# Summed weight blocks of a two-level FFN product: accumulating transfers into the SBUF chunk in place of sums staged in DRAM

## The chip, the cores and the metric

The kernel runs on one core of a Trainium2 chip. The metric is the device time of one execution in microseconds (us). Before the change it is 1157.83 us (median of 3 runs, 1157.72 to 1158.13).

## The reference, cut to what matters

One layer of a hybrid decoder for 576 tokens (64 new ones of 8 sequences and 512 of a prompt, side by side in one tile): two recurrent branches, a cross-attention, and a SwiGLU FFN. The change touches only how the FFN's input weights arrive:

```
xn = rms_norm(x, g[4])                          # 576 x 1024
gate, up = jnp.split(xn @ w_ffn_in, 2, axis=-1) # w_ffn_in: 1024 x 5632, each half 1024 x 2816
x = x + rms_norm((jax.nn.silu(gate) * up) @ w_ffn_out, g[5])
```

All matrix products are float32 work done as three matmuls on parts of the operands: a weight is split into a high part (`whi`, by ScalarE) and the rest (`wlo`, by VectorE), and so are the activations.

## The kernel before, in words

Weights come through one stream. `w_cols` and `w_blocks` register the chunks in the order in which they will be used; `w_dma` fetches a chunk from DRAM into one of five `wraw` buffers (128 x 1024 float32, 512 KB) by transfers that SyncE issues (L187; the trace shows them at L185); `w_prep` or `w_part` splits it into `whi` and `wlo` (4 buffers each). In the stage around the change, `run_steps` splits the chunk that stands three behind the one in use. SyncE has its own instruction stream, so a fetch waits for nothing but its buffer: chunk n goes out when chunk n-5 has been split.

Column block j is 128 columns of gate and 128 of up, 22 blocks in all. The first 7 (`NB`) are computed plainly. For the other 15, `ffn_pair` computes gate and up for both halves of the tokens (288 columns L, 288 columns R) with seven products in place of eight, in the manner of Strassen and Winograd. Each product takes four 128 x 128 weight blocks, thus 12 matmuls on 288 columns (L1395 to L1397). The weights of a product are EG, OG, EU, OU (even and odd row blocks of gate or up), or a sum of those: s1 = EU + OU, s2 = EG + EU + OU, s3 = EG + EU, s4 = EG + OG + EU + OU. The seven products come in the order EG, s1, s2, OG, s3, s4, OU; each needs 256 KB of weights, and two products in a row share a chunk. Below, a *pair* is a chunk with its two products. Blocks 7 to 13 make 49 products in 25 pairs (part 1), blocks 14 to 21 make 56 in 28 pairs (part 2). Ahead of each part stand eight steps of `ffo_part`, the output product on the columns of the part before, during which the first chunks of the part are fetched and split. In these stages the order on TensorE, ScalarE and VectorE is as written in the code.

The sums s1 to s4 are made earlier in DRAM: 32 transfers of 960 KB (`sum_task`, L557) that GpSimd issues between the steps of the recurrent branches, from 35 us to 385 us. A "copy" writes a sum's first term, an "add" accumulates another (`accum_op`). 16 tiny GpSimd copies into `small` (L758, L779) hold GpSimd's queue to the pace of the steps. In the FFN, `block` then fetches a finished sum from DRAM as it fetches any other block.

GpSimd's DMA queue works in order: a transfer whose wait isn't met holds back all that stand behind it.

Of the kernel before, what the change touches and what calls it, by code (L numbers as in the profile page):

```python
# [9 lines left out]
F32 = mybir.dt.float32  # L10
F32R = mybir.dt.float32r
AF = mybir.ActivationFunctionType
ALU = mybir.AluOpType
# [8 lines left out]
DFF = 2816  # L22
# [5 lines left out]
NB = 7  # L28
# [24 lines left out]
def decoder_step(  # L53
# [7 lines left out]
    nc = tc.nc  # L61
    PE, ACT, DVE, POOL = nc.tensor, nc.scalar, nc.vector, nc.gpsimd
# [38 lines left out]
    def split(hi, lo, src):  # L101
        ACT.copy(hi, src)  # L102
        DVE.tensor_sub(lo, src, f(hi))  # L103
# [74 lines left out]
    def w_dma(upto):  # L178
        while ptr["dma"] <= min(upto, len(wsrc) - 1):
            i = ptr["dma"]  # L180
            srcs, nk, ncol, _ = wsrc[i]
            t = wraw_p.tile([128, 1024], F32, tag="wraw", name="wraw")
            n = nk * ncol // len(srcs)
            for j, src in enumerate(srcs):
                nc.sync.dma_start(out=t[:, j * n:(j + 1) * n].rearrange("p (k c) -> p k c", c=ncol), in_=src)  # L185
            raw[i] = t
            ptr["dma"] += 1  # L187

# [2 lines left out]
    def w_part(i, b, dma_ahead=2):  # L191

        if i >= len(wsrc) or (b == 0 and ptr["prep"] > i) or (b == 1 and i not in parts):
            return
        assert b or ptr["prep"] == i
        w_dma(i + dma_ahead)
        _, nk, ncol, as_is = wsrc[i]
        if as_is or nk * ncol < 1024:
            if b == 0:
                w_prep(i)  # L200
            return
        if b == 0:
            ptr["prep"] += 1
            t = raw.pop(i)
            hi = whi_p.tile([128, 1024], F32R, tag="whi", name="whi")
            lo = wlo_p.tile([128, 1024], F32R, tag="wlo", name="wlo")
            parts[i] = t, hi, lo
            ready[i] = hi.rearrange("p (k c) -> p k c", c=ncol), lo.rearrange("p (k c) -> p k c", c=ncol)
        t, hi, lo = parts[i] if b == 0 else parts.pop(i)
        s = slice(b * 512, b * 512 + 512)  # L210
        split(hi[:, s], lo[:, s], t[:, s])
# [30 lines left out]
    def drain(budget=None):  # L242
        spent = 0
        while bg and (budget is None or spent < budget):
            c, fn = bg.popleft()
            if fn is NEXT:
                if budget is not None:
                    return
                continue
            with tc.high_priority(offset=PRIO):  # L250
                fn()
            spent += c

    def step(w, pe, post=None, budget=4000, prep=True):
        steps.append((w, pe, post, budget, prep))

    def run_steps():
        nextw = 0
        manual = ExitStack()
        by_hand = False  # L260
        for w, pe, post, budget, prep in steps:
            if w:
                nextw = w[-1] + 1
            if prep in ("pair", "hand"):
                if not by_hand:
                    by_hand = True
                    drain(None)
                    w_prep(nextw - 1 + 2)
                    manual.enter_context(tc.manual_schedule(engines={PE.engine, ACT.engine, DVE.engine}))
                pe(*[ready.pop(i) for i in w])  # L270
                soon, late = post or (None, None)
                if soon:
                    soon()
                if prep == "pair":
                    w_part(nextw - 1 + 3, 0 if w else 1)
                else:
                    w_prep(nextw - 1 + 3)
                if late:
                    late()
                continue  # L280
            if not prep:
                pe()
            else:
                w_prep((w[0] if w else nextw) + 3)
                pe(*[ready.pop(i) for i in w])
            if post:
                post()
            drain(budget)
        manual.close()
# [13 lines left out]
    small = cst.tile([128, 80], F32, name="small")  # L303
# [237 lines left out]
        return g  # L541

    sums = {n: tc.dram_tile([512, DFF - NB * 128], F32, name=f"sum_{n}") for n in ("s1", "s2", "s3", "s4")}

    def sum_task(op, n, src, i):
        def go():
            r = slice(i * 128, i * 128 + 128)
            if src in sums:  # L550
                a = sums[src][r, :]
            else:
                k = 2 * i + (src[0] == "O")
                c = (src[1] == "U") * DFF
                a = w_ffn_in[0][k * 128:(k + 1) * 128, c + NB * 128:c + DFF]
            kw = {"accum_op": ALU.add} if op == "add" else {}
            tc.keep_in_program_order(nc.gpsimd.dma_start(out=sums[n][r, :], in_=a, **kw))  # L557
        return go

    sum_tasks = deque(  # L560
        sum_task(op, n, src, i)
        for stage in ((("copy", "s1", "EU"), ("copy", "s3", "EG")), (("add", "s1", "OU"), ("add", "s3", "EU")),
                      (("copy", "s2", "s3"),), (("add", "s2", "OU"),), (("copy", "s4", "s2"),), (("add", "s4", "OG"),))
        for op, n, src in stage for i in range(4))

    def sum_step():
        if sum_tasks:
            step([], sum_tasks.popleft(), budget=0)


    h_h, h_l, vv = [None] * KT, [None] * KT, [None] * KT
    box = {}

# [142 lines left out]
    for c in range(KT):  # L716
        def wi(sec):
            return [w_cols(w_in[0], 0, KT, sec * D + c * 128, 128)]
        if c == 0:
            wi(3), wi(1)  # L720
            step([1], startup, lambda: (in_u(0)[1](), in_hc(0)[1](), softplus()), budget=0, prep=False)
        else:
            step(wi(3), *in_u(c), budget=0)
            step(wi(1), *in_hc(c), budget=3000)
        if c:
            sum_step()
        step(wi(2), *in_hh(c), budget=2000)
        if c:
            sum_step()
        step([], *in_gate(c), budget=2000)  # L730
        step(wi(0), *in_hb(c), budget=9000)
        if c:
            sum_step()


    vs_h, vs_l, z1 = [None] * KT, [None] * KT, [None] * KT
# [12 lines left out]
    def br_rnn(n):  # L749
        def pe(W):  # L750
            box["yr"] = mmt()
            gemm2(box["yr"], W, full(h_h, h_l))

        def post():
            t = box.pop("sgs")
            DVE.tensor_mul(both(t), both(t), box.pop("yr")[:, :, :HN])
            z1[n] = t
            POOL.tensor_copy(small[:, n:n + 1], t[:, 0:1])  # L758
            vs_h[n], vs_l[n] = new(F32R), new(F32R)
            split(vs_h[n][:, :T], vs_l[n][:, :T], vv[n][:, :T])  # L760
            free(vv[n])
            if n == 0:
                free(gd, gr_a, gr_x)
            if n == KT - 1:
                free(h_h, h_l)
        return pe, post
# [3 lines left out]
    def br_conv(n):  # L770
        def pe(W):
            box["yc"] = mmt()
            gemm2(box["yc"], W, full(vs_h, vs_l))

        def post():
            t = box.pop("sgs")
            DVE.tensor_mul(both(t), both(t), box.pop("yc")[:, :, :HN])
            DVE.tensor_add(t[:, :T], t[:, :T], z1[n][:, :T])
            POOL.tensor_copy(small[:, n:n + 1], t[:, 0:1])  # L779
            z_h[n], z_l[n] = new(F32R), new(F32R)  # L780
            split(z_h[n][:, :T], z_l[n][:, :T], t[:, :T])
            free(t, z1[n])
            if n == KT - 1:
                free(vs_h, vs_l, xn_h, xn_l)
        return pe, post
# [18 lines left out]
    for n in range(KT):  # L804
        step([w_cols(w_in[0], 0, KT, 5 * D + n * 128, 128)], *br_gate(n, "r"))
        step([w_cols(w_rnn_out[0], 0, KT, n * 128, 128)], *br_rnn(n))
        if n == 1:
            step([], state_out)
        sum_step()
    for n in range(KT):  # L810
        step([w_cols(w_in[0], 0, KT, 4 * D + n * 128, 128)], *br_gate(n, "c"))
        step([w_cols(w_conv_out[0], 0, KT, n * 128, 128)], *br_conv(n))
        sum_step()
    assert not sum_tasks


    fb = [[None] * 2 for _ in range(4)]
# [201 lines left out]
    for h in (h0, h1):  # L1019
        for n in range(KT):  # L1020
            step([w_cols(w_mix_out[0], 0, KT, n * 128, 128)], *proj_half(n, fullh(z_h, z_l), h, 1, after_mix),
                 budget=BUD["mix"])
# [337 lines left out]
    def ffn_half(j, up, h):  # L1360
# [15 lines left out]
            free(t)  # L1376
        return pe, post

    def block(name, j):
        if name in sums:  # L1380
            src = sums[name][:, (j - NB) * 128:(j - NB + 1) * 128].rearrange("(k p) c -> p k c", p=128)
        else:
            c = (name[1] == "U") * DFF + j * 128
            src = w_ffn_in[0][:, c:c + 128].rearrange("(k e p) c -> e p k c", p=128, e=2)[name[0] == "O"]
        return src

    FF = {}

# [354 lines left out]
```

## Time and profile before

| | |
|---|---|
| median of 3 runs | 1157.83 us (1157.72 to 1158.13) |
| profiled execution | 1157.59 us, of which the profile's span 1155.8 us |
| TensorE busy | 1134.3 us, 98% of the span |
| VectorE, ScalarE, GpSimd busy | 58%, 52%, 13% |
| chain that ended last | TensorE 94% |
| DMA, SyncE's queue (q1) | 249812 packets, 149.95 MB, 43.6% of 16 engines' time |
| DMA, GpSimd's queue (q0) | 6144 packets, 38.50 MB, 13.0% |

Matmuls are pipelined: one that the profile shows with 295 ns starts 132 ns after the one before. The pace of TensorE is therefore read from the starts, not from the durations. Transfers show twice: as the short time in which they are issued, and as the time "to landing", from issue until the semaphore says that all is in place. GpSimd's issue time of a transfer isn't counted in its busy time.

### The profile page before, as it was taken

The page shows a single profiled execution, that of the slowest core. Times are in us where ns is not written, and L with a number is a line of the kernel's source. Part 1 is how long each engine was busy: PE and PEld are TensorE (multiplying, and loading weights), DVE is VectorE, ACT ScalarE, POOL GpSimd, SP SyncE. Part 2 cuts the span into 40 slices and gives each one's busy share as a digit, 9 for nine tenths or more (in the row PEclk, how much of TensorE's full clock was granted, in tenths as well). Part 3 has the DMA queues.
Part 4 walks back from the last instruction along what each step waited for, and adds up shares of the span by engine and source line. Part 5 has one row for each costly group of instructions (what it writes and reads, how often), then busy time and mean ns, then how long its engine had stood idle before and what let it go on. Part 6 is the DMA issues. An engine that isn't in the chain of part 4 may idle for free.

```text
span 1155.8 us, 21040 instructions
## 1 busy us (share of the span) xinstructions
PE 1134.3 (98%) x8524; PEld 1113.9 (96%) x8524; DVE 675.0 (58%) x1082; ACT 603.2 (52%) x1030; POOL 146.9 (13%) x301
## 2 busy tenths in 40 slices
PE   6999999999999999999999999999999999999996
PEld 4999999999999999999998899999999999999996
DVE  6666666652223335698767777989314663466535
ACT  5665566652122225666557778775325552255543
POOL 4433333212001000022210000000000000000000
PEclk9999999999999999999999999999999999999999
DMA  7556787567547546567675585565444553455702
GB/s 226 171 163 191 178 186 163 177 160 170 173 141 164 147 123 187 147 193 227 196 227 189 192 274 165 155 200 164 129 126 131 164 150 107 118 164 166 227 2 83
DMA packets 256859, 191.13 MB, mean 165 GB/s; under 512 B 9432, under 2 KB 241896, under 8 KB 256634
## 3 DMA queue, kind: packets, MB, share of 16 engines
q1 hardware_dynamic: 249812, 149.95, 43.6%
q0 software_dynamic: 6144, 38.50, 13.0%
q8 instruction: 67, 1.10, 0.4%
q10 hardware_dynamic: 806, 1.34, 0.3%
q14 instruction: 30, 0.25, 0.1%
HBM read 180.36 MB, written 40.85 MB: 191 GB/s over the span
## 4 chain that ended last, share of the span: by engine, by line
PE 94%; DVE 2%; ACT 1%; DMA 1%; issue 1%; POOL 0%; SPq 0%; DVEq 0%; ACTq 0%
PE mm L107 23%; PE mm L108 23%; PE mm L106 23%; PE aux L1397 4%; PE aux L1396 4%; PE aux L1395 4%; PE aux L1225 1%; PE aux L1209 1%; PE aux L106 1%; PE aux L107 1%; PE aux L108 1%; PE mm L1397 1%; PE mm L1396 1%; PE mm L1395 1%; DMA wraw<-in_w_in_dram 1%
## 5 line engine op out<-in xcount | busy, mean ns | idle before, releaser
L106 PE MATMUL mm<-u,whi 128*128 128x288 f32 (+2 forms) x2032 | 605.3, 298 | 0.6 <-ACT u L458 0.6
L107 PE MATMUL mm<-u,whi 128*128 128x288 f32 (+2 forms) x2032 | 601.7, 296 | 0.5 <-DVE u L103 0.5
L108 PE MATMUL mm<-u,wlo 128*128 128x288 f32 (+2 forms) x2032 | 601.7, 296 | 0.2 <-POOL wlo L431 0.2
L103 DVE TENSOR_TENSOR wlo<-wraw,whi 128x1024 fp32r<-128x1024 f32 (+2 forms) x294 | 304.0, 1035 | 215.5 <-ACT whi L102 209.1
L102 ACT CAST whi<-wraw 128x1024 fp32r<-128x1024 f32 (+2 forms) x294 | 261.1, 898 | 286.6 <-PE mm L107 216.6
L107 PEld LDWEIGHTS mm<-u,whi 128*128 128x128 f32 x2032 | 384.5, 189 | 2.4 <-DVE u L103 1.3
L106 PEld LDWEIGHTS mm<-u,whi 128*128 128x128 f32 x2032 | 384.3, 189 | 2.2 <-ACT u L458 1.2
L108 PEld LDWEIGHTS mm<-u,wlo 128*128 128x128 f32 x2032 | 384.0, 189 | 0.8 <-POOL wlo L431 0.6
L1397 PE MATMUL aux<-u,wlo 128*128 128x288 f32 x360 | 106.2, 295 | 0.0
L1396 PE MATMUL aux<-u,whi 128*128 128x288 f32 x360 | 106.1, 295 | 0.0
L1395 PE MATMUL aux<-u,whi 128*128 128x288 f32 x360 | 105.9, 294 | 0.0
L102 ACT CAST u<-u 128x576 fp32r<-128x576 f32 (+6 forms) x117 | 58.9, 532 | 78.6 <-DVE u L640 26.2
L103 DVE TENSOR_TENSOR u<-u,u 128x576 fp32r<-128x576 f32 (+6 forms) x117 | 65.4, 578 | 16.8 <-ACT u L102 16.6
L1397 PEld LDWEIGHTS aux<-u,wlo 128*128 128x128 f32 x360 | 67.6, 188 | 0.0
L1395 PEld LDWEIGHTS aux<-u,whi 128*128 128x128 f32 x360 | 67.6, 188 | 0.0
L1396 PEld LDWEIGHTS aux<-u,whi 128*128 128x128 f32 x360 | 67.6, 188 | 0.0
L103 DVE TENSOR_TENSOR u<-aux,u 128x512 fp32r<-128x512 f32 (+2 forms) x60 | 32.8, 584 | 3.9 <-ACT u L102 3.8
L102 ACT CAST u<-aux 128x512 fp32r<-128x512 f32 (+2 forms) x60 | 28.0, 514 | 6.6 <-DVE u L103 2.1
L106 PE MATMUL aux<-u,u 128*128 128x256 f32 (+1 forms) x96 | 27.8, 294 | 0.0
L108 PE MATMUL aux<-u,u 128*128 128x256 f32 (+1 forms) x96 | 27.7, 289 | 0.0
L107 PE MATMUL aux<-u,u 128*128 128x256 f32 (+1 forms) x96 | 27.6, 289 | 0.0
L1425 ACT ACTIVATE u<-u 128x576 f32<-128x576 f32 x15 | 10.3, 686 | 32.9 <-DVE u L1422 32.9
(284 smaller groups left out, 1193.2 us busy)
## 6 DMA issues: line engine op xcount, KB each, us to landing
wraw<-in_w_in_dram SPq DMA_DIRECT2D x48, 512.0 KB, 4.1
sum_s<-in_w_ffn_in_dram POOLq DMA_DIRECT2D x24, 960.0 KB, 8.3
wraw<-sum_s SPq DMA_DIRECT2D x60, 256.0 KB, 3.3
wraw<-in_w_ffn_in_dram SPq DMA_DIRECT2D x28, 512.0 KB, 4.8
wraw<-in_w_ffn_in_dram SPq DMA_DIRECT2D x45, 256.0 KB, 3.3
wraw<-in_w_mix_out_dram SPq DMA_DIRECT2D x16, 512.0 KB, 3.8
wraw<-in_w_kv_x_dram SPq DMA_DIRECT2D x16, 512.0 KB, 3.8
wraw<-in_w_q_x_dram SPq DMA_DIRECT2D x16, 512.0 KB, 3.9
```

What stands on the lines that cost most here:

```text
L102: ACT.copy(hi, src)
L103: DVE.tensor_sub(lo, src, f(hi))
L106: PE.matmul(out, lhsT=wh, rhs=xh, start=start, stop=False)
L107: PE.matmul(out, lhsT=wh, rhs=xl, start=False, stop=False)
L108: PE.matmul(out, lhsT=wl, rhs=xh, start=False, stop=stop)
L1209: PE.transpose(ps[:, d * 256 + i * 128:d * 256 + (i + 1) * 128], kr[i][:, h * 256 + d * 128:h * 256 + (d + 1) * 128], ident)
L1225: PE.matmul(ps[0:m], lhsT=t[:, k * 64:k * 64 + m], rhs=src, **kw)
L1395: PE.matmul(ps, lhsT=wh[:, k, :], rhs=xh[x][:, xs], start=first and i == 0, stop=False, skip_group_check=True)
L1396: PE.matmul(ps, lhsT=wh[:, k, :], rhs=xl[x][:, xs], start=False, stop=False, skip_group_check=True)
L1397: PE.matmul(ps, lhsT=wl[:, k, :], rhs=xh[x][:, xs], start=False, stop=last and i == 3, skip_group_check=True)
L1425: ACT.activation(FF["t"][:, 0:T], FF["t"][:, 0:T], AF.Silu)
```

## The change

The staging in DRAM, its 32 transfers and the 16 copies into `small` are gone. `block` now returns a list of parts; `w_dma` fetches the first part with SyncE as before, and adds each further part onto it in SBUF by a transfer of GpSimd's with `accum_op` (256 KB in 128 x 4 runs of 128 floats). Per column block these are 1 (s1), 2 (s2), 1 (s3) and 3 (s4): 7 adds, 105 in all. The split of pairs asks `w_dma` for chunks up to 4 ahead in place of 2.

```
@@ w_dma
-                nc.sync.dma_start(out=t[:, j * n:(j + 1) * n].rearrange("p (k c) -> p k c", c=ncol), in_=src)
+                dst = t[:, j * n:(j + 1) * n].rearrange("p (k c) -> p k c", c=ncol)
+                src = src if isinstance(src, list) else [src]
+                nc.sync.dma_start(out=dst, in_=src[0])
+                for more in src[1:]:
+                    nc.gpsimd.dma_start(out=dst, in_=more, accum_op=ALU.add)
@@ run_steps
-                    w_part(nextw - 1 + 3, 0 if w else 1)
+                    w_part(nextw - 1 + 3, 0 if w else 1, 4)
@@ sum_task, sum_tasks, sum_step
-    sums = {n: tc.dram_tile([512, DFF - NB * 128], F32, name=f"sum_{n}") for n in ("s1", "s2", "s3", "s4")}
...
-            kw = {"accum_op": ALU.add} if op == "add" else {}
-            tc.keep_in_program_order(nc.gpsimd.dma_start(out=sums[n][r, :], in_=a, **kw))
...
@@ steps of the branches (eight places)
-        sum_step()
@@ br_rnn, br_conv
-            POOL.tensor_copy(small[:, n:n + 1], t[:, 0:1])
@@ block
+    PARTS = {"s1": ("EU", "OU"), "s2": ("EG", "EU", "OU"), "s3": ("EG", "EU"), "s4": ("EG", "OG", "EU", "OU")}
+
     def block(name, j):
-        if name in sums:
-            src = sums[name][:, (j - NB) * 128:(j - NB + 1) * 128].rearrange("(k p) c -> p k c", p=128)
-        else:
-            c = (name[1] == "U") * DFF + j * 128
-            src = w_ffn_in[0][:, c:c + 128].rearrange("(k e p) c -> e p k c", p=128, e=2)[name[0] == "O"]
-        return src
+
+        def src(part):
+            c = (part[1] == "U") * DFF + j * 128
+            return w_ffn_in[0][:, c:c + 128].rearrange("(k e p) c -> e p k c", p=128, e=2)[part[0] == "O"]
+        return [src(p) for p in PARTS.get(name, (name,))]
```

The rows on TensorE, ScalarE and VectorE are the same before and after, but for line numbers. On SyncE the same fetches stand in the same places, from `w_ffn_in` where they came from `sum_s`.

GpSimd before, late in the branches (`sum_s_96` is s2, `sum_s_98` is s4; what a row waits for stands in brackets, DMASW being GpSimd's own transfers, DMAHW those of SyncE):

```order
L758 COPY small<-u_3133 128x1 [waits DVE_49]
L557 DMA sum_s_96<-in_w_ffn_in_dram 128x1920 [waits DMASW3_49]
L758 COPY small<-u_3252 128x1 [waits DVE_49]
L557 DMA sum_s_98<-sum_s_96 16x15360 [waits DMASW4_49]
L758 COPY small<-u_3371 128x1 [waits DVE_49]
L557 DMA sum_s_98<-sum_s_96 16x15360 [waits DMASW5_49]
```

All of these rows are gone; GpSimd goes from the state outputs straight to the transfers of the mixing stage.

GpSimd before, from the last transfers ahead of the FFN pairs to the end (`x2a_s` and `x_s` are spills of tokens to DRAM):

```order
L1317 DMA x2a_s<-u_8626 128x640 [waits DMASW7_49,DVE_49,Activation_49]
L1473 DMA x_s<-u_9745 128x512 [waits DMASW0_49,Activation_49]
L1473 DMA x_s<-u_9804 128x512 [waits DMASW1_49,Activation_49]
L1473 DMA x_s<-u_9863 128x512 [waits DMASW2_49,Activation_49]
L1473 DMA x_s<-u_9923 128x512 [waits DMASW3_49,Activation_49]
L1739 UNCONDITIONAL_BRANCH
```

GpSimd now, in the same place (L1440 is the spill, L189 the adds; the transfers take the semaphores DMASW0 to DMASW7 in turn, so the spill on DMASW5 is followed by adds on DMASW6 and DMASW7):

```order
L1440 DMA x_s<-u_9811 128x512 [waits DMASW5_49,Activation_49]
L189 DMA wraw<-in_w_ffn_in_dram 128x4x128 [waits DMAHW6_49,DMAHW2_49,DMAHW7_49,DMASW6_49,DVE_49]
L189 DMA wraw<-in_w_ffn_in_dram 128x4x128 [waits DMAHW7_49,DMASW7_49]
L1440 DMA x_s<-u_9872 128x512 [waits DMASW0_49,Activation_49]
L189 DMA wraw<-in_w_ffn_in_dram 128x4x128 [waits DMASW7_49,DMASW1_49]
L189 DMA wraw<-in_w_ffn_in_dram 128x4x128 [waits DMASW2_49,DMASW1_49]
L189 DMA wraw<-in_w_ffn_in_dram 128x4x128 [waits DMAHW2_49,DMAHW1_49,DVE_49]
L189 DMA wraw<-in_w_ffn_in_dram 128x4x128 [waits DMAHW3_49,DMASW4_49]
L189 DMA wraw<-in_w_ffn_in_dram 128x4x128 [waits DMASW5_49,DMASW4_49]
```

The first two adds are those of s3 and the first of s4, each waiting for its plain fetch (DMAHW); the next two are the second and third of s4, each waiting for the add before it (DMASW7, then DMASW1); then come s1 and the two adds of s2 of the next column block, the last of which waits for the one before (DMASW4). Blocks in the same chunk don't wait for each other.

## Rows read from the trace of the kernel before

**Rows 1.** Busy time by stretch: one of the branches, then part 1 and part 2.
```profile
core 0: us, PE busy (x) PEld busy (x) DVE busy (x) ACT busy (x) POOL busy (x), PEclk, DMA share, GB/s
35.00:130.00 95.00, 95.00 (x717) 94.66 (x716) 61.23 (x98) 57.62 (x86) 34.99 (x83) 1.00 0.58 172
...
877.40:954.60 77.20, 77.20 (x586) 77.20 (x585) 49.44 (x85) 42.45 (x81) 0.00 (x0) 1.00 0.55 159
1000.40:1088.90 88.50, 88.50 (x671) 88.50 (x670) 58.64 (x102) 48.40 (x94) 0.00 (x0) 1.00 0.57 166
```

**Rows 2.** TensorE in order of time (start, duration): first matmul of parts and after.
```profile
877.54 0.29 PE L1395 MATMUL aux<-u,whi 128*128 128x288 f32 x1
...
955.38 0.30 PE L106 MATMUL mm<-u,whi 128*128 128x288 f32 x1
...
1000.30 0.29 PE L1395 MATMUL aux<-u,whi 128*128 128x288 f32 x1
...
1089.25 0.31 PE L106 MATMUL mm<-u,whi 128*128 128x320 f32 x1
```

**Rows 3.** SyncE in order of time: the first fetches for parts 1 and 2.
```profile
840.09 5.96 SPq L185 DMA_DIRECT2D wraw<-sum_s  x2
...
851.69 0.91 SPq L185 DMA_DIRECT2D wraw<-sum_s  x2
...
863.69 0.92 SPq L185 DMA_DIRECT2D wraw<-sum_s  x2
...
869.97 5.50 SPq L185 DMA_DIRECT2D wraw<-sum_s  x2
...
963.76 5.53 SPq L185 DMA_DIRECT2D wraw<-sum_s  x2
...
991.72 5.49 SPq L185 DMA_DIRECT2D wraw<-sum_s  x2
```

**Rows 4.** The page's DMA issues: count, KB each, median us to landing.
```profile
sum_s<-in_w_ffn_in_dram POOLq DMA_DIRECT2D x24, 960.0 KB, 8.3
wraw<-sum_s SPq DMA_DIRECT2D x60, 256.0 KB, 3.3
...
sum_s<-sum_s POOLq DMA_DIRECT2D x8, 960.0 KB, 5.2
...
x_s<-u POOLq DMA_DIRECT2D x8, 256.0 KB, 3.1
```

**Rows 5.** DMA queues and issues in 358 to 371 us: one accumulating transfer.
```profile
q0 software_dynamic: 144, 0.98, 36.7%
...
sum_s<-in_w_ffn_in_dram POOLq DMA_DIRECT2D x1, 960.0 KB, 8.4
```

**Rows 6.** The same in 306 to 319 us: one plain copy from DRAM to DRAM.
```profile
q0 software_dynamic: 32, 0.98, 22.6%
```

**Rows 7.** GpSimd in order of time: add, dependent copy with its wait, add, spill.
```profile
193.64 0.80 POOL L557 DMA_DIRECT2D sum_s<-in_w_ffn_in_dram  x1
...
202.56 0.53 POOL L557 DMA_DIRECT2D sum_s<-sum_s  x1 [6.49 <-DMA sum_s<-in_w_ffn_in_dram]
...
319.85 0.49 POOL L557 DMA_DIRECT2D sum_s<-sum_s  x1 [0.27 <-issue]
...
851.32 0.54 POOL L1473 DMA_DIRECT2D x_s<-u  x1 [5.47 <-ACT u L1472]
```

**Rows 8.** ScalarE in order of time: splits of the last s4 blocks of parts 1 and 2.
```profile
943.96 0.60 ACT L102 CAST whi<-wraw 128x512 fp32r<-128x512 f32 x1
...
1077.84 0.60 ACT L102 CAST whi<-wraw 128x512 fp32r<-128x512 f32 x1
```

**Rows 9.** DMA queue of SyncE in 1005 to 1080 us: packets, MB, share of 16 engines.
```profile
q1 hardware_dynamic: 25041, 12.46, 57.2%
```

**Rows 10.** Busy time by stretch, as Rows 1: the last 6 us, after TensorE's work.
```profile
1150.00:1156.00 6.00, 0.00 (x0) 0.00 (x0) 2.55 (x4) 0.00 (x0) 0.00 (x0) 0.56 0.47 175
```

More of the change, by code (lines that the diff above doesn't have):

```diff
@@ L541, in gate_w @@
         return g
-    sums = {n: tc.dram_tile([512, DFF - NB * 128], F32, name=f"sum_{n}") for n in ("s1", "s2", "s3", "s4")}
[L547 to L551, printed above, removed]
-            else:
-                k = 2 * i + (src[0] == "O")
-                c = (src[1] == "U") * DFF
-                a = w_ffn_in[0][k * 128:(k + 1) * 128, c + NB * 128:c + DFF]
-            kw = {"accum_op": ALU.add} if op == "add" else {}
-            tc.keep_in_program_order(nc.gpsimd.dma_start(out=sums[n][r, :], in_=a, **kw))
[L558 to L568, printed above, removed]
     h_h, h_l, vv = [None] * KT, [None] * KT, [None] * KT
@@ L724, in decoder_step @@
             step(wi(1), *in_hc(c), budget=3000)
-        if c:
-            sum_step()
         step(wi(2), *in_hh(c), budget=2000)
-        if c:
-            sum_step()
         step([], *in_gate(c), budget=2000)
         step(wi(0), *in_hb(c), budget=9000)
-        if c:
-            sum_step()
     vs_h, vs_l, z1 = [None] * KT, [None] * KT, [None] * KT
@@ L778, in post @@
             DVE.tensor_add(t[:, :T], t[:, :T], z1[n][:, :T])
-            POOL.tensor_copy(small[:, n:n + 1], t[:, 0:1])
             z_h[n], z_l[n] = new(F32R), new(F32R)
@@ L808, in decoder_step @@
             step([], state_out)
-        sum_step()
     for n in range(KT):
@@ L812, in decoder_step @@
         step([w_cols(w_conv_out[0], 0, KT, n * 128, 128)], *br_conv(n))
-        sum_step()
-    assert not sum_tasks
     fb = [[None] * 2 for _ in range(4)]
@@ L1377, in ffn_half @@
         return pe, post
+    PARTS = {"s1": ("EU", "OU"), "s2": ("EG", "EU", "OU"), "s3": ("EG", "EU"), "s4": ("EG", "OG", "EU", "OU")}
     def block(name, j):
-        if name in sums:
-            src = sums[name][:, (j - NB) * 128:(j - NB + 1) * 128].rearrange("(k p) c -> p k c", p=128)
-        else:
-            c = (name[1] == "U") * DFF + j * 128
-            src = w_ffn_in[0][:, c:c + 128].rearrange("(k e p) c -> e p k c", p=128, e=2)[name[0] == "O"]
-        return src
+        def src(part):
+            c = (part[1] == "U") * DFF + j * 128
+            return w_ffn_in[0][:, c:c + 128].rearrange("(k e p) c -> e p k c", p=128, e=2)[part[0] == "O"]
+        return [src(p) for p in PARTS.get(name, (name,))]
     FF = {}
```

## The prediction

> **What bounds the kernel now.** I read the busy time by stretch first. TensorE is busy without a gap in a stretch in which the staging runs (95.00 of 95.00 us) and in both parts of the pairs (77.20 of 77.20, 88.50 of 88.50) [rows 1]. So nothing that is taken off the DMA engines or GpSimd in the branches can shorten them: the gain side of this change is near 0. What counts is whether the new transfers keep up with TensorE in the pairs. Its pace there: part 1 runs from 877.54 to 955.38, 77.84 us for 49 products, part 2 from 1000.30 to 1089.25, 88.95 us for 56 [rows 2], that is 1.59 us a product, **11.1 us per column block**, 22.2 us per two blocks.
>
> **What goes.** 32 staging transfers (24 + 8) [rows 4] and the 16 copies into `small`, all beside a TensorE that doesn't wait [rows 1]: 0 us, with 0 to 1 us of gain as bounds, since the stretches have no idle time to give.
>
> **What doesn't change.** The orders on TensorE, ScalarE, VectorE and SyncE. Asking 4 chunks ahead puts no fetch earlier: SyncE's fetches stand in the same order and each waits for the buffer of the chunk five before. 60 of the 105 fetches have another source, of the same size. 0 us.
>
> **What is added: 7 adds per column block in GpSimd's queue.** That queue is in order. By the order rows, s1's add, the first of s2's, s3's and the first of s4's wait only for plain fetches; the second add of s2 and the second and third of s4 each wait until the add before has landed, and all behind them wait along. With I the time GpSimd needs to issue an add, and A the time from an add's issue to its landing, a block costs the queue: s1 I, s2 A + I, s3 I, s4 2A + I, together **4I + 3A**. GpSimd has no other work there (0.00 us busy [rows 1]).
>
> *I.* The adds of before take 0.80 us to issue, the copies 0.49 to 0.54 [rows 7], for 128 rows. The new ones have 512 runs. If time goes by transfer, I is 0.8; if the extra 0.3 us goes by runs, 0.5 + 4 x 0.3 = 1.7. I take the middle, 1.3.
>
> *A.* No add of 256 KB into SBUF is in this trace. Nearest rows: a plain fetch of 256 KB in the same 512-byte runs lands in 3.3 us, a copy of 256 KB by GpSimd in 3.1 [rows 4]; the 960 KB add in 8.4 [rows 5], the 960 KB copy in 5.2 [rows 4], with fetches beside both. The wait before a dependent copy agrees: add issued at 193.64, copy let go at 202.56, 8.9 us [rows 7]. Lower bound: an add is as quick as a plain fetch, 3.3. Upper: it takes what the 960 KB add takes, 8.4, if its four times as many pieces cost what its bytes save. I take the fetch times the ratio of add and copy, 3.3 x 8.4 / 5.2 = 5.3.
>
> So a block costs 4 x 1.3 + 3 x 5.3 = **21.1 us against TensorE's 11.1**: GpSimd's queue becomes the bound.
>
> **The sum, part 1.** What is saved by early work must be counted. Chunk by chunk, from the fetches [rows 3], each landing 3.3 us after issue: s1 goes out at 840.1, its add is issued about 843.4 and the queue is free at 844.7. s2's fetch (the second of the row at 840.09, about 845.6) lands at 848.9; its adds go at 848.9 and 854.2, free at 855.5; a spill of 0.5 us [rows 7] stands next. s3 and s4 (fetched at 851.69) go 856.0, 857.3, 862.6, 867.9; free at 869.2, when the second block's s1 and s2 (863.69) are there: 869.2, 870.5, 875.8; then s3 877.1, and s4 (the second of the row at 869.97, about 875.1) 878.4, 883.7, 889.0. After two blocks the queue is free at 890.3. From there it is never without work, since four chunks lie fetched ahead: 5 x 21.1 = 105.5 brings it to 995.8, and the last add of the last s4, issued at 994.5, lands at 999.8. ScalarE split that block at 943.96 [rows 8], so it comes 55.8 us late. ScalarE's queue stands on that split; TensorE can run about one further pair's work before it needs a bank that ScalarE must empty, less the time of those copies: about 2 us. Part 1: +54.
>
> **Part 2.** The queue empties during `ffo_part`, and starts afresh in a frame shifted by 54. In the times of before: s1's add at 967.1, s2's fetch lands at 972.2 [rows 3], and in the same way the queue is free of two blocks at 1013.1 (the second s4's fetch, about 996.8, is in time). 6 x 21.1 = 126.6 gives 1139.7; the last add lands at 1143.7, where ScalarE split the block at 1077.84 [rows 8]: 65.9 late, less 2. Part 2: +64.
>
> Sum: 1157.6 for the profiled execution (0.2 below the median of the runs) + 54 + 64 = **1275 us**. The same chunk-by-chunk sum with I 0.8 and A 3.3 (13.1 a block) gives +10 and +11, less 4: 1175. With 1.8 and 8.4 (32.4 a block) it gives +137 and +158, less 4: 1449.
>
> TensorE's clock could add to that. After its last matmul the granted clock of the final 6 us is 0.56 [rows 10], near the lower of its two levels (1.2 and 2.4 GHz), and here it would wait some 10 us per block. At half clock 11.1 us of products become 22.2, just over the queue's 21.1: mostly hidden, at worst 1.1 x 15 = 16 us, 1291. I leave it to the range.
>
> A rule that speaks against the change: the Trainium skill's page "Collectives: The Full Stack", section "The bandwidth ceiling: the fold count and why AG ≠ RS ≠ AR", explains a halved rate of reductions by two source reads for each add. The trace agrees in direction: one 960 KB add holds the engines for 36.7% of 13 us, 4.8 us [rows 5], one copy for 22.6%, 2.9 us [rows 6]. By twice a fetch's 0.90 us [rows 9], 14 adds and 14 fetches per two blocks would need 37.8 us of all engines, 7.8 us a block over TensorE's pace: 117 less 32, 1243.
>
> **Rivals.**
> *The engines, not the chain, set the pace (chance 0.12).* Adds land so fast that the queue's waits are short, but the engines are full. 25041 packets take 57.2% of 75 us [rows 9], 42.9 us for 12.46 MB, 47.5 times 256 KB: 0.90 us for each, 12.6 us per two blocks of 14. An add by its bytes takes 4.8 x 256/960 = 1.28, 14 of them 17.9 us. Sum 30.5 against 22.2: 4.2 us a block, 62 us for 15, less the 32 us that the early chunks save in the sum above (15 x 10.0 - 118): +30, 1188. For it: adds of different blocks can overlap. Against: three of seven can't.
> *Runs cost as much as bytes (0.12).* Four times as many pieces per byte; A is 8.4 or more: 1449 and up. Against: packets of 512 bytes take 42.9 x 16 / 25041 = 27 ns in plain fetches [rows 9], so time goes by bytes there.
> *All of it is hidden: not slower (0.05).* If I is 0.54 as for a copy [rows 7] and A below (11.1 - 4 x 0.54) / 3 = 3.0 us, the queue keeps TensorE's pace and the time stays 1157.6. The point of decision is an A of 3.0 us, and an add's engine time of (22.2 - 12.6) / 14 = 0.69 us. Against: a plain fetch lands in 3.3, and an add's bytes alone need 1.28. The Trainium skill's page "DMA: Bandwidth & Descriptors", section "Anatomy of one DMA", gives 2.0 us plus bytes over 436 GB/s for a transfer by GpSimd: 2.6 us here, which is this rival. For the 960 KB add that rule makes 4.3 us where the row has 8.4 [rows 5], so I give it little.
> *Faster (0.02).* The DMA relief in the branches would have to show in a TensorE that has no gap there.
>
> **How the numbers follow.** Chain of adds 0.69, at 1275, its own range 1200 to 1390 (I from 0.9 to 1.7, A from 4.0 to 7.0). With the others, 1190 to 1400 leaves out the hidden case, the fast ones, and most of the case of costly runs, 2 in 10. A measurement of this kernel can tell 0.2%, 2.3 us. Faster 0.02; same 0.05, the hidden case; slower 0.93.
>
> **What would show it.** Right: TensorE without a gap until about 877, then idle about half of each column block, with ScalarE's splits of `wraw` waiting on transfers from `w_ffn_in`; GpSimd's waits nearly all on its own adds; part 1 some 130 us long, part 2 some 150; adds landing in about 5 us. The engines as the bound would show a DMA share near 1 throughout the pairs. Wrong: adds landing under 3 us, or a chain that overlaps where I make it wait; I would also be wrong if an add of 512 runs takes GpSimd several us to issue, which would push the time above the range.

## The result and the profile after

The changed kernel takes **1317.1 us** (median of 4 runs, 1313.55 to 1319.91) against 1157.98 for the kernel before (1157.72 to 1158.52): ratio 1.1372, 95% interval 1.1342 to 1.1402. Measured once more beside the last experiments it gave 1323.6 and 1.1431 (1.1413 to 1.1448). Forecast were 1275 and a range of 1190 to 1400. The mechanism is the one forecast; its size came out 42 us above the forecast. The profiled execution has a span of 1318.1 us, 162.3 over that of before.

Busy time by stretch, after, with the columns of [rows 1]: part 1, the output steps between, part 2. The column of GpSimd (POOL) does count the time in which it issues transfers: the 40 and 47 in it are adds.

```profile
877.00:1030.00 153.00, 95.74 (x606) 93.67 (x606) 49.98 (x87) 43.27 (x82) 52.05 (x40) 0.81 0.88 155
1030.00:1076.00 46.00, 45.85 (x346) 45.61 (x346) 16.21 (x20) 8.44 (x10) 11.67 (x9) 1.00 0.74 142
1076.00:1252.00 176.00, 106.58 (x671) 103.80 (x670) 58.05 (x104) 48.63 (x96) 61.15 (x47) 0.81 0.89 159
```

Both parts now hold idle TensorE time (57 and 69 us) where [rows 1] had none, and the granted clock in them falls from 1.00 to 0.81. The eight steps between the parts stay almost without a gap (45.85 of 46). So the loss is in the pairs. TensorE in order of time (start, duration) answers to [rows 2]:

```profile
878.41 0.29 PE L1362 MATMUL aux<-u,whi 128*128 128x288 f32 x1
...
1250.52 0.31 PE L106 MATMUL mm<-u,whi 128*128 128x320 f32 x1
```

Part 1 starts 0.9 us later than before. The step behind part 2 starts at 1250.52 where it was 1089.25: 161.3 us later. (Part 2 starts at 1074.21, so part 1 with the steps behind it cost 73.9 and part 2 87.4.) The longest waits from 870 us on: who waited at which line, for whom, us, times, the longest.

```profile
POOL wraw L189 <- DMA wraw<-in_w_ffn_in_dram: 234.7, 44, 26.9
DVE wlo L103 <- ACT whi L102: 212.9, 53, 11.4
ACT whi L102 <- DMA wraw<-in_w_ffn_in_dram: 200.3, 35, 11.9
...
PE aux L1362 <- ACT u L1373: 117.3, 13, 11.5
```

Read from below, this is the path: TensorE waits 13 times, in 15 column blocks, for a bank that ScalarE has to empty (L1373); ScalarE stands in its queue on a split (L102) whose chunk has not landed; and GpSimd (L189) holds the next add back until the one before has landed. GpSimd in order of time over part 1 (start, time of the issues in a row, their count, idle time before them):

```profile
867.69 1.27 POOL L189 DMA_DIRECT2D wraw<-in_w_ffn_in_dram  x1 [7.13 <-DMA wraw<-in_w_ffn_in_dram]
872.32 3.91 POOL L189 DMA_DIRECT2D wraw<-in_w_ffn_in_dram  x3 [3.36 <-DMA wraw<-in_w_ffn_in_dram]
881.79 3.94 POOL L189 DMA_DIRECT2D wraw<-in_w_ffn_in_dram  x3 [5.55 <-DMA wraw<-in_w_ffn_in_dram]
893.21 1.29 POOL L189 DMA_DIRECT2D wraw<-in_w_ffn_in_dram  x1 [7.48 <-DMA wraw<-in_w_ffn_in_dram]
899.88 3.90 POOL L189 DMA_DIRECT2D wraw<-in_w_ffn_in_dram  x3 [5.39 <-DMA wraw<-in_w_ffn_in_dram]
...
1013.55 1.28 POOL L189 DMA_DIRECT2D wraw<-in_w_ffn_in_dram  x1 [3.43 <-DMA wraw<-in_w_ffn_in_dram]
...
1095.08 3.91 POOL L189 DMA_DIRECT2D wraw<-in_w_ffn_in_dram  x3 [4.59 <-DMA wraw<-in_w_ffn_in_dram]
...
1234.15 1.28 POOL L189 DMA_DIRECT2D wraw<-in_w_ffn_in_dram  x1 [5.17 <-DMA wraw<-in_w_ffn_in_dram]
```

899.88 is the last add of the second block of part 1, 1013.55 that of the seventh: five blocks in 113.7 us, **22.7 us a block**. In part 2 it is 1095.08 to 1234.15 for six blocks, **23.2**. TensorE's pace was 11.1. ScalarE's splits of the last s4 blocks answer to [rows 8]: 943.96 and 1077.84 became

```profile
1018.05 0.62 ACT L102 CAST whi<-wraw 128x512 fp32r<-128x512 f32 x1 [9.56 <-DMA wraw<-in_w_ffn_in_dram]
...
1238.75 0.62 ACT L102 CAST whi<-wraw 128x512 fp32r<-128x512 f32 x1 [10.25 <-DMA wraw<-in_w_ffn_in_dram]
```

The queues in 900 to 990 us (packets, MB, share of 16 engines; q0 carries the adds, q1 the fetches), with the issues of that stretch and its busy time; then all adds of the kernel: ns of an issue (min, median, max), who waited for them (us, times), their landing.

```profile
q0 software_dynamic: 14764, 7.34, 66.3%
q1 hardware_dynamic: 14240, 7.07, 28.7%
...
wraw<-in_w_ffn_in_dram POOLq DMA_DIRECT2D x29, 256.0 KB, 6.2
wraw<-in_w_ffn_in_dram SPq DMA_DIRECT2D x27, 256.0 KB, 3.9
...
900.00:990.00 90.00, 54.35 (x336) 52.97 (x336) 29.55 (x52) 24.48 (x48) 37.60 (x29) 0.79 0.95 160
...
L189 POOL DMA_DIRECT2D wraw<-in_w_ffn_in_dram x105: 1267/1681/2437, 845.9 to 1234.2; - x105
...
  POOL wraw L189: 216.3, 45
...
DMA to landing us min/median/max: 4.3/6.0/9.5
```

An add lands 6.0 us after its issue (median). Its issue takes 1.28 us where it stands alone; in a row an issue begins before the one before has ended, so its record is longer (median 1.68), and three in a row take 3.9 together. The packets of an add take 0.663 x 90 / 29 = **2.06 us** of all 16 engines, those of a fetch of the same size 0.287 x 90 / 27 = **0.96**. Together the queues' shares make 0.95. That does not yet mean that the engines are full. A share adds up the times of all packets, and where the engines are busy in every slice, below, the sum is 1.30 with adds (e2) and 1.10 with copies (e7): packets overlap in time. By what they move the engines stand at 160 GB/s here against 202 in e2. Still, two bounds lie close to each other, and the experiments have to part them.

### The profile page after: what moved, and what is told of

Its sections match the earlier page's. It is cut to its first block, busy times and chain, and to the rows that moved or that the text cites. A ratio compares the mean times of both kernels' runs of the same rounds, so it can differ in the third digit from the quotient of the medians.

```text
span 1318.1 us, 21168 instructions
## 1 busy us (share of the span) xinstructions
PE 1166.2 (88%) x8524; PEld 1141.1 (87%) x8524; DVE 675.3 (51%) x1082; ACT 601.8 (46%) x1030; POOL 254.8 (19%) x358
## 3 DMA queue, kind: packets, MB, share of 16 engines
q0 software_dynamic: 57872, 34.57, 18.5%
## 4 chain that ended last, share of the span: by engine, by line
PE 66%; issue 13%; DMA 10%; POOL 6%; DVE 3%; ACT 2%; SPq 0%; POOLq 0%; DVEq 0%; ACTq 0%
PE mm L107 19%; PE mm L108 19%; PE mm L106 19%; DMA wraw<-in_w_ffn_in_dram 9%; POOL wraw L189 6%; PE aux L1191 1%; PE aux L1175 1%; PE aux L106 1%; PE aux L108 1%; PE aux L107 1%; DVE wlo L103 1%; DMA u<-in_x_prompt_dram 1%; DMA wraw<-in_w_o_x_dram 0%; DVE u L103 0%; PE aux L923 0%
## 5 line engine op out<-in xcount | busy, mean ns | idle before, releaser
L102 ACT CAST whi<-wraw 128x1024 fp32r<-128x1024 f32 (+2 forms) x294 | 262.1, 899 | 478.4 <-PE mm L107 212.9
L1362 PE MATMUL aux<-u,whi 128*128 128x288 f32 x360 | 118.0, 328 | 126.7 <-ACT u L1373 117.3
L1362 PEld LDWEIGHTS aux<-u,whi 128*128 128x128 f32 x360 | 75.6, 210 | 131.5 <-ACT u L1373 120.3
L189 POOL DMA_DIRECT2D wraw<-in_w_ffn_in_dram x105 | 136.9, 1664 | 256.3 <-DMA wraw<-in_w_ffn_in_dram 248.2
L1363 PE MATMUL aux<-u,whi 128*128 128x288 f32 x360 | 114.9, 319 | 0.0
L1364 PE MATMUL aux<-u,wlo 128*128 128x288 f32 x360 | 114.7, 319 | 0.0
L102 ACT CAST u<-u 128x576 fp32r<-128x576 f32 (+6 forms) x117 | 58.8, 531 | 67.5 <-DVE u L617 26.3
L1363 PEld LDWEIGHTS aux<-u,whi 128*128 128x128 f32 x360 | 76.3, 212 | 0.0
L1364 PEld LDWEIGHTS aux<-u,wlo 128*128 128x128 f32 x360 | 76.2, 212 | 0.0
L933 POOL DMA_DIRECT2D x_s<-u x8 | 4.5, 560 | 226.9 <-DVE u L924 226.6
L102 ACT CAST u<-aux 128x512 fp32r<-128x512 f32 (+2 forms) x60 | 28.0, 515 | 6.4 <-DVE u L103 2.1
L106 PE MATMUL aux<-u,u 128*128 128x256 f32 (+1 forms) x96 | 27.8, 295 | 0.0
L108 PE MATMUL aux<-u,u 128*128 128x256 f32 (+1 forms) x96 | 27.6, 288 | 0.0
```

Of the source, the lines that this page charges most:

```text
L106: PE.matmul(out, lhsT=wh, rhs=xh, start=start, stop=False)
L108: PE.matmul(out, lhsT=wl, rhs=xh, start=False, stop=stop)
L189: nc.gpsimd.dma_start(out=dst, in_=more, accum_op=ALU.add)
L933: nc.gpsimd.dma_start(out=x1_s[p, h, :, :2 * HW[h]], in_=fb[p][h][:, :2 * HW[h]])
L1362: PE.matmul(ps, lhsT=wh[:, k, :], rhs=xh[x][:, xs], start=first and i == 0, stop=False, skip_group_check=True)
L1363: PE.matmul(ps, lhsT=wh[:, k, :], rhs=xl[x][:, xs], start=False, stop=False, skip_group_check=True)
```

## The experiments

Theory: GpSimd's in-order queue, which stands still while a dependent add lands (4I + 3A a block). Rival: the DMA engines, which move four fifths of what they move in e2.

**e1_no_adds.** Is the removal worth anything, and are the adds the whole loss? The adds are left out.

```
-                for more in src[1:]:
-                    nc.gpsimd.dma_start(out=dst, in_=more, accum_op=ALU.add)
```

> The 105 adds are left out (each summed block holds only its first part), all else as after the change. Every theory puts the whole loss on the adds and no gain on the removed staging: 1157 to 1159 us, TensorE without a gap in the pairs. If the removal of the staging and of the copies into small were worth something, the time would lie below 1156.

Measured: 1158.22 us, ratio 1.0003 (0.9993 to 1.0012). Taking the staging out of the branches gains nothing, and the whole loss comes with the adds.

**e2_free_chain.** No add waits for another: the second and third of a sum go to three spare tiles in turn.

```
+                for q, more in enumerate(src[1:]):
+                    to = dst
+                    if q:
...
+                        to = spare[ptr["spare"] % len(spare)].rearrange("p (k c) -> p k c", c=ncol)
...
+                    tc.keep_in_program_order(nc.gpsimd.dma_start(out=to, in_=more, accum_op=ALU.add))
```

> The second and third adds of s2 and s4 go onto three spare tiles in turn, so that no add has to wait for the one just before it; all 105 adds keep their size and their runs, and the queue keeps program order. (The sums s2 and s4 are left incomplete.) Chain theory (GpSimd's queue waits for landings, 4I + 3A = 23 us a block): the queue costs 7 x 1.3 = 9.1 us a block, under TensorE's 11.1, so 1158 to 1180. Engine theory (the 16 DMA engines are full: 7 x 2.06 us for adds and 7 x 0.96 for fetches = 21.1 us a block): the time stays high, 10 x 15 - 32 = +118, about 1276, with a DMA share near 1 in the pairs.

Measured: 1231.57 us, ratio 1.0632 (1.0616 to 1.0648), between the two theories. Its engines and queues in 900 to 950 us (busy tenths in 40 slices, then as above):

```profile
DMA  9999999999999999999999999999999999999999
...
q0 software_dynamic: 10183, 5.05, 79.3%
q1 hardware_dynamic: 10107, 5.02, 50.7%
```

And GpSimd in order of time, two adds that stand 14 apart in its queue, thus two blocks:

```profile
1059.95 1.28 POOL L199 DMA_DIRECT2D wraw<-in_w_ffn_in_dram  x1 [3.71 <-DMA wraw<-in_w_ffn_in_dram]
...
1096.25 1.28 POOL L199 DMA_DIRECT2D wraw<-in_w_ffn_in_dram  x1 [3.86 <-DMA wraw<-in_w_ffn_in_dram]
```

Without the chain the engines are full in every slice, none of GpSimd's waits is for one of its own adds any more, and a block takes 36.3 / 2 = 18.1 us. That is the second bound: 7 adds and 7 fetches need 18.1 us of all engines, still 7 over TensorE's 11.1. Breaking the chain gives back 85.5 us; 73.6 stay.

**e3_short_s4.** Fewer adds: s4 made of two parts, 5 adds a block (two of its four terms are left out).

```
-    "s4": ("EG", "OG", "EU", "OU")
+    "s4": ("EG", "OG")
```

> s4 is made of EG and OG alone: two of the seven adds of a block are gone, both of them in the chain (s4 is left incomplete). Chain theory: 4I + A = 4 x 1.3 + 6.0 = 11.2 us a block, about TensorE's pace: 1158 to 1170. Engine theory: 5 x 2.06 + 7 x 0.96 = 17.0 us a block, +88 less about 32 of early work: about 1214.

Measured: 1207.98 us, ratio 1.0424 (1.0405 to 1.0444), close to the engines' figure. By the starts of its adds a block takes 16.4 us in part 1 and 15.5 in part 2, where the one wait that is left would make 4 x 1.28 + 6.8 = 11.9. So the engines decide here in the main: in 900 to 960 us q0 has 71.1% and q1 39.8%, together above 1, and the adds land in 6.8 us (median).

**e4_plain_copies.** The same transfers, order and waits, but plain copies.

```
-                    nc.gpsimd.dma_start(out=dst, in_=more, accum_op=ALU.add)
+                    nc.gpsimd.dma_start(out=dst, in_=more)
```

> The 105 transfers of GpSimd's copy in place of adding (the last part overwrites the sum), with the same waits, order, size and runs. Chain theory with a copy's landing of 3.1 to 4.2 us and an issue of about 1.0: 13 to 17 us a block, 1165 to 1215. Engine theory: 14 x 0.96 = 13.4 us a block, 1158 to 1170. What lies between this and 1317 is the price of accumulating itself.

Measured: 1234.79 us, ratio 1.0659 (1.0642 to 1.0677), above what either theory gave. The queues in 900 to 960 us with the issues of that stretch:

```profile
q1 hardware_dynamic: 13136, 6.53, 41.5%
q0 software_dynamic: 1969, 6.42, 35.0%
...
wraw<-in_w_ffn_in_dram POOLq DMA_DIRECT2D x25, 256.0 KB, 4.3
```

The shares add up to 0.77 only, so here the chain binds in the main: an issue takes 0.75 us, a landing 4.3, and 4 x 0.75 + 3 x 4.3 = 15.9 us a block. The starts of the copies give 17.6 and 17.8: the 45 that are waited for landed in 4.7 on average, and some of the rest is waits for other things. Even with copies the kernel is 77 us over the one before; the accumulation adds 82 to that. The packets of a copy take 0.350 x 60 / 25 = 0.84 us of the engines, less than half of an add's.

**e7_free_plain.** Both taken away: e2's spare tiles with e4's copies.

```
-                    tc.keep_in_program_order(nc.gpsimd.dma_start(out=to, in_=more, accum_op=ALU.add))
+                    tc.keep_in_program_order(nc.gpsimd.dma_start(out=to, in_=more))
```

> Copies instead of adds, and the second and third of a block go to three spare tiles, so that none waits for the one before: neither the accumulation nor the chain is left, only 105 further transfers of 256 KB. Fetch and copy together need about 7 x (0.9 + 0.9) = 12.6 us of the engines a block, against TensorE's 11.1. Two bounds: 1160 to 1190. If the queue's issue or the count of transfers were the cause, it stays near the 1235 of the copies with waits.

Measured: 1171.19 us, ratio 1.0111 (1.0093 to 1.0130), as expected of two bounds. Busy time in 900 to 950 us:

```profile
900.00:950.00 50.00, 46.55 (x348) 45.86 (x347) 29.98 (x55) 25.05 (x48) 20.84 (x28) 1.00 1.10 291
```

The engines are busy in every slice again (291 GB/s against 202 in e2), but 105 more copies cost only 13 us. The four runs make a square (us):

| | adds | copies |
|---|---|---|
| each waits for the one before | 1317.1 | 1234.8 |
| no waits among them | 1231.6 | 1171.2 |

The chain costs 86 us with adds and 64 with copies; accumulating costs 82 with the chain and 60 without. Neither alone is the cause, and each makes the other dearer: together they cost 146, where 64 and 60 would make 124.

**e5_staggered.** The real sums, in another order: of six adds that depend on an earlier one (two blocks), five stand three or four adds behind it and one, s4's second of every other block, only two. `WHEN` says for each chunk of seven and each half of it how many chunks later, and at which place there, an add is issued.

```
+    WHEN = {(0, 1): [(0, 1)], (1, 0): [(0, 1), (1, 2)], (2, 0): [(0, 3)], (2, 1): [(0, 0), (2, 0), (3, 1)],
+            (4, 0): [(0, 1)], (4, 1): [(0, 2), (1, 2)], (5, 1): [(0, 0)], (6, 0): [(0, 1), (2, 0), (3, 1)]}
```

> All 105 adds with their real operands and targets, but in another order in GpSimd's queue: an add that depends on an earlier one is issued at least three adds after it, between adds of other blocks, so that the landing is mostly over when its turn comes. Nothing is left out. If the loss is two bounds close to each other (the queue's waits at 23 us a block, and under them the engines at 18.1 us a block, which the run with spare targets showed), this falls to that second bound: 1225 to 1250 us. If the waits for landings are no cause of their own (the run with spare targets was quick because its second and third adds went to other tiles), it stays at 1300 to 1320. If only the waits were the cause, 1158 to 1180.

Measured: 1272.78 us, ratio 1.0997 (1.0975 to 1.1018): the waits are a cause, but only half of what e2 gave back comes back. GpSimd's waits by releaser, in us and times, and (the last line) its waits on its own adds, which were 216.3 us in 45:

```profile
  DMA wraw<-in_w_ffn_in_dram: 155.8, 33
  DVE wlo L103: 17.0, 5
...
  POOL wraw L183: 37.8, 14
```

Its waits have moved from its own adds to other things: plain fetches above all (155.8 less 37.8), and splits that empty a buffer. A likely reading, not tested by itself: a chunk whose last add is issued up to three chunks later holds one of five buffers longer, while e2's chunks were ready after their first add.

**e6_long_runs.** Does an add cost by its pieces? 128 runs of 2 KB in place of 512 of 512 bytes (other weights are summed).

```
-                for more in src[1:]:
-                    nc.gpsimd.dma_start(out=dst, in_=more, accum_op=ALU.add)
+                for q, more in enumerate(src[1:]):
+                    r = 128 * (ptr["dma"] % 8)
+                    nc.gpsimd.dma_start(out=t[:, j * n:(j + 1) * n], in_=w_ffn_in[0][r:r + 128, q * 512:q * 512 + 512],
+                                        accum_op=ALU.add)
```

> The 105 adds read 128 runs of 2 KB of w_ffn_in in place of 512 runs of 512 B: the same bytes, waits and order, other weights are summed. If the price of an add goes by its pieces (one piece about 65 ns of an engine, an issue that writes 512 of them), the issue falls from 1.28 to 0.6 to 0.8 us, the landing from 6.0 to 4 to 5 us, a block to some 17 us: 1215 to 1250 us. If it goes by bytes, issue and landing stay and so does the time: 1305 to 1325.

Measured: 1292.81 us, ratio 1.1162 (1.1146 to 1.1179), nearer to "by bytes". The adds, ns of an issue (min, median, max) and us to landing, and the queue in 900 to 990 us with 31 adds:

```profile
L190 POOL DMA_DIRECT2D wraw<-in_w_ffn_in_dram x105: 863/941/1595, 846.1 to 1208.5; - x105
...
DMA to landing us min/median/max: 4.1/5.7/9.7
...
q0 software_dynamic: 4327, 7.87, 57.7%
```

With about a quarter of the packets an add's take 0.577 x 90 / 31 = 1.68 us of the engines, against 2.06. So most of an add's price goes with its bytes, not with its pieces. (These adds also read the same 24 blocks of DRAM again and again; that is not parted here.)

**e10_half_adds.** Does it go by size at all? Each add carries half of its block (the other half of each sum is left out).

```
-                    nc.gpsimd.dma_start(out=dst, in_=more, accum_op=ALU.add)
+                    nc.gpsimd.dma_start(out=dst[:, 0:2], in_=more[:, 0:2], accum_op=ALU.add)
```

> Each add carries two of a block's four row groups: 128 KB in 256 runs; the other half of each sum is left out. It splits issue and landing into a fixed part and one that goes with the size. If both halve (0.65 and 3.0 us), a block takes 4 x 0.65 + 3 x 3.0 = 11.6 us on GpSimd's queue and the time is 1158 to 1185. If half of the landing is fixed (4.5 us), a block takes 16.1 us: 1205 to 1230. If the landing stays near 6, 20.6 us: 1275 to 1300.

Measured: 1250.19 us, ratio 1.0792 (1.0775 to 1.0808), between the second and the third figure.

```profile
L189 POOL DMA_DIRECT2D wraw<-in_w_ffn_in_dram x105: 1172/1207/2237, 844.4 to 1163.5; - x105
...
DMA to landing us min/median/max: 3.4/4.7/6.9
```

Half the bytes still take 1.21 us to issue (1.28 whole) and 4.7 to land (6.0). 4 x 1.21 + 3 x 4.7 = 18.9 us a block; the starts of the adds give 18.5 and 19.2. From 512 runs to 256 the issue hardly falls. Over half of the landing does not go with the size: with 6.0 = f + s and 4.7 = f + s/2, f is 3.4 and s 2.6, an estimate, and s is at most that, since half the bytes also load the engines less.

**e8_ahead2 and e11_after_again.** Is asking four chunks ahead worth anything? e8 asks for two; e11 is the changed kernel again.

```
-                    w_part(nextw - 1 + 3, 0 if w else 1, 4)
+                    w_part(nextw - 1 + 3, 0 if w else 1)
```

> The pairs ask for their chunks two ahead in place of four; all else as in the changed kernel. If, as the prediction says, the fetches are held by the buffer of the chunk five before, the time is the changed kernel's within 0.5% (1310 to 1324). If the four chunks ahead hide part of the chain, it is 10 to 40 us slower.

> The changed kernel once more, to stand beside the run that asks for chunks two ahead (1326 us), since that was on another chip than the first measurement of the changed kernel. If four ahead hides part of the chain, this is again 5 to 12 us below 1326: 1314 to 1321. If the difference is the chip's, it is 1322 to 1330.

Measured: e8 1325.73 us, ratio 1.1440 (1.1422 to 1.1458); e11 1323.6, ratio 1.1431 (1.1413 to 1.1448). The intervals overlap: nothing is seen of the four chunks ahead. What looked like 9 us against the first measurement of the changed kernel is within what that kernel itself shows from one measurement to the next; these two runs were on different chips as well.

**e9_onchip_sums.** Is it building the sums late that costs, or the way they are added? The same sums in the same chunks, added by GpSimd's own vector unit from blocks that lie in SBUF, the memory on the chip. A block needs 6 fetches and no transfer of GpSimd's.

```
+        if name == "s1":
...
+            nc.sync.dma_start(out=dst, in_=part("EU"))
+            nc.sync.dma_start(out=other.rearrange("p (k c) -> p k c", c=128), in_=part("OU"))
+            POOL.tensor_add(flat, flat, other)
+        elif name == "s3":
+            nc.sync.dma_start(out=dst, in_=part("EU"))
+            POOL.tensor_add(flat, flat, held["EG", j])
+        elif name == "s2":
+            POOL.tensor_add(flat, held["EG", j], held["s1", j])
+        elif name == "s4":
+            POOL.tensor_add(flat, held["s2", j], held["OG", j])
```

> The same sums, built in the same SBUF chunks when they are needed and not staged in DRAM, but added by GpSimd's vector unit from blocks that are in SBUF already: s1 is EU plus a fetched OU, s2 = EG + s1, s3 = a fetched EU + EG, s4 = s2 + OG. Per column block 6 fetches (7 before) and 4 additions of 128x512, at half of the 2.8 us that GpSimd takes for 128x1024 some 1.4 us each, 5.6 us against TensorE's 11.1. Nothing is left out. If the loss is the accumulating transfers (their price on the engines and the wait for landings), the time is that of the kernel before: 1156 to 1162; not quicker, since TensorE had no gap. If building the sums late is the cause, whatever adds them, it is well over 1180.

Measured: 1160.3 us (11 runs), ratio 1.0017 (1.0009 to 1.0026). Both parts and the steps between:

```profile
870.00:960.00 90.00, 89.53 (x675) 89.07 (x673) 63.35 (x91) 46.82 (x86) 34.27 (x23) 1.00 0.47 136
960.00:1000.00 40.00, 40.00 (x305) 40.00 (x304) 14.25 (x14) 6.92 (x7) 10.20 (x8) 1.00 0.30 88
1000.00:1095.00 95.00, 94.96 (x713) 94.42 (x712) 74.92 (x106) 51.38 (x99) 37.28 (x25) 1.00 0.51 149
```

TensorE has next to no gap again, at full clock, with GpSimd busy about two fifths of the time in the parts. So the sums can be made when they are needed; it was the accumulating transfers that cost. The profile pages also put the traffic of the DRAM (HBM) at 145 MB read and 9.4 written, where the kernel before had 180 and 41. It is not faster than before: TensorE's work is the floor of these stages in both, so no version of this edit that leaves that work as it is could have beaten the old kernel by the pairs. It is 2 us over. Matmul by matmul against the kernel before, TensorE is 0.6 us late before the pairs, as it is in e1, and 1.8 behind them; why the pairs take 1.3 longer with next to no gap stays open.

## Why the prediction was right, and by how much it was short

- *What goes is worth 0: right.* e1, 1.0003. From 35 to 395 us q0 falls from 36.2% to 0.3% of the engines, and TensorE stays at 95.00 of 95.00 in the stretch of [rows 1].
- *Orders and the four chunks ahead are worth 0: right*, by e8 and e11.
- *The queue's law 4I + 3A: right in kind, and so near in number partly by luck.* With the measured 1.28 and 6.0 it gives 23.1 us a block; measured were 22.7 and 23.2, and GpSimd waited on its own adds 45 times, three a block. But 6.0 is the median of all adds: the 45 that another one waits for landed in 6.6 on average, each taken from the trace. And the queue is not quite the one of the sum: in 14 of the 45 cases an independent add stands between the two, so that its issue falls into the wait. The two nearly cancel.
- *I = 1.3: the value right (1.28), its reason only in part.* It was the middle between two guesses, by transfer and by runs, so the hit is luck. 256 runs take 1.21, 128 long ones 0.9, and a copy of 512 runs 0.75 (e10, e6, e4): runs and accumulation both count, and neither in proportion.
- *A = 5.3: the term that was mis-sized.* Measured is a median of 6.0, and it is no constant. In the GpSimd rows an add that stands alone lets the next go after 1.27 + 3.36 = 4.6 us (issued at 867.69); the third of three in a row only after 1.3 + 7.48 = 8.8 (the row of 881.79), a little of it because its issue had to stand behind two others. I took A from a transfer that stood alone and from fetches beside fetches; here the adds share the engines, mostly with themselves. The median rises with that load: 6.0 here, 10.2 with the engines full (e2).
- *The early work: too cheap, for the same reason.* The 14th add of part 1 was to be issued at 889.0 and was at 899.88, +10.9; that of part 2, shifted by part 1's 73.9, was to come at 1085.7 and came at 1095.08, +9.4.
- *The sum.* Forecast +118, measured +161.3. The early blocks take 20.3 of the difference, five blocks of 1.6 and six of 2.1 take 20.6; the 2.4 that are left lie at the starts and ends of the parts, where the clock has a share (next point).
- *The clock: hidden within the parts, not at their ends.* After a wait of 8.43 us TensorE's matmuls take 0.44 us and later 0.29, and the parts' mean granted clock is 0.81. Within a part the period of a block is already the queue's, and GpSimd waits for no matmul, so there is little room for the clock in it. Behind the last add of a part nothing hides it. In the first stretch after the last wait of each part (8.14 and 6.86 us, rows below) the granted clock is 0.50, the lower of its two levels, and TensorE starts a matmul every 0.24 us in place of 0.13. That is some 4 us for both ends together, about what the forecast had taken off for TensorE's running ahead. No run took the clock alone away.

```profile
1019.60:1023.10 3.50, 3.50 (x14) 3.50 (x15) 1.15 (x2) 0.98 (x3) 0.00 (x0) 0.50 0.62 183
...
1240.30:1245.10 4.80, 4.80 (x20) 4.80 (x21) 2.42 (x4) 2.80 (x7) 0.00 (x0) 0.50 0.39 109
```

- *The rival of the engines: wrong as the cause of this time, nearer than I made it.* At 18.1 us a block (e2) it lies 5 under the chain, where I had 15.25. My price of an add, 1.28 us by the bytes of the 960 KB add, was the error: its packets take 2.06 of the engines. Nor could the sign that I had set for this rival, a DMA share near 1, part the two: it is 0.88 and 0.89 in the parts, but 1.30 where the engines do bind. The Trainium skill's page "Collectives: The Full Stack", section "The bandwidth ceiling: the fold count and why AG ≠ RS ≠ AR", has two source reads for each add of a collective's reduction. The trace agrees in size, though no run shows the reads themselves: 2.06 is 2.1 times a fetch's 0.96, and the 18.9 us a block that I worked out by that rule stand beside the 18.1 of e2.
- *The hidden case: wrong*, as weighed. An A of 3.0 was the point of decision; the fastest add of the changed kernel took 4.3, the fastest copy in an add's place 3.2 (e7). The rule of the Trainium skill's page "DMA: Bandwidth & Descriptors", section "Anatomy of one DMA", gave an estimate of 2.6 us; the measurement decides against it here.

## What to carry to other kernels

A chain of dependent transfers in an in-order queue costs its landings one after the other, not its bytes: count issues and landings along the queue before counting bandwidth. Price an accumulating transfer at the load that it will itself make, and keep the second bound beside the first, since repairing the chain alone (e5, e2) gave back a quarter to a half of the loss. Where the operands pass through SBUF anyway, a vector unit with time to spare adds them without any of this (e9).

## What the runs showed of the hardware that was not expected

- Accumulating about doubles what a transfer asks of the engines: its packets take 2.06 us for 256 KB against 0.84 for a copy (e4) and 0.96 for a fetch; with both queues full the core moved 202 GB/s with adds (e2) and 291 with copies (e7), from which an add comes out at some 1.7 us where a fetch or a copy takes 0.9 (an estimate that counts fetch and copy alike).
- GpSimd's copies of 512-byte runs go in fewer packets: 1969 for 25 copies (e4), some 79 each, where 29 adds took 14764, some 509 each. An add keeps about a packet for each run, in e6 too (4327 for 31 adds of 128 runs).
- An add's issue hardly depends on its size: 1.21 us for 128 KB in 256 runs, 1.28 for 256 KB in 512; 256 KB in 128 runs of 2 KB take 0.9 (e6).
